# A rebuilt opening, row norms and gate tiles over both halves in a hybrid S5, convolution and ConvFFN trunk

## The chip, the cores and the metric

The kernel runs on 1 core of one Trainium2 chip. The metric is the time of one execution on the device in microseconds (us); of several runs the median is given. The core has five engines that each take their own instructions strictly in order: TensorE (PE, the matrix engine), VectorE (DVE), ScalarE (ACT), GpSimd (POOL) and SyncE (SP, which here issues DMA transfers). Engines wait for each other with semaphores. PE writes its results into PSUM, which here is cut into eight banks of 128 x 512 numbers.

## The reference, cut to what matters

The model has two layers and runs on a prompt of 1040 tokens (16 of them fixed "meta" tokens) and 8 samples of 4 tokens. Each layer has a mixer and a ConvFFN with a causal depthwise convolution of width 3. The change lies in the mixer of the first layer:

```python
xn = rms_norm(x, p['norm_mix'][l])
z = xn @ p['w_in_even'][i]                      # 1024 -> 2048
u_a, x_b, g_b, g_c = jnp.split(z, [512, 1024, 1536], axis=-1)
y_a, nh_re, nh_im = s5_scan(u_a, ...)           # complex diagonal state space, 32 groups x 64 states
y_a = jax.nn.gelu(y_a)
y_a = y_a * jax.nn.sigmoid(y_a @ w_glu + b_glu)
conv, nbuf = causal_dwconv(g_c * x_b, sbuf, p['w_sconv'][i])   # width 3
y_b = g_b * conv
out = jnp.concatenate([y_a, y_b], axis=-1) @ p['w_out_even'][i]
```

The second layer's mixer is a Conformer convolution module of width 31 with two 1024-wide products and a layer norm. Both ConvFFNs have an inner width of 2816. All is float32.

## The kernel before, in words

**Tokens.** The 1072 tokens are laid along the free dimension, features on the 128 partitions. They are cut into two halves of 512 and 560. Half 0 fills one PSUM bank; half 1 is done as two blocks of 280 in two banks.

**Products.** A float32 product is made from three faster ones. A weight tile (128 x 1024, 512 KB) is loaded by SP into `raw`, copied by ACT into its high part `wh`, and DVE or POOL subtracts to get the low part `wl` (`weight`, lines 105 to 116; a counter hands out the subtractions). The activations are split alike into `xnh` and `xnl`, with the norm's gain as a scale (`split`, lines 136 to 145). `dense` (line 118) then runs over the eight tiles of 128 input features and, for each, issues xh.wh, xl.wh and xh.wl: 24 matmuls of 512 columns for half 0, 48 of 280 columns for half 1 (line 126). The row norm is not applied before a product but when its result is read out of PSUM (`evac`, which multiplies by `rstd`).

**The opening.** `prepare` (line 275) splits each x tile, squares it on ACT, and adds the squares up on DVE (half 0) or POOL (half 1). `inv_std` then multiplies the sum by ones on PE (`nrm`, line 196), computes the inverse root on DVE, puts it on a diagonal `dg`, and PE spreads it over the partitions (`bcs`, line 213). Four tiles of `z` hold u_a; `u_tile` (line 368) makes them in the order `ORDER_U`, each tile and half on its own, and writes them to DRAM (`du`), from where they come back group by group.

**S5.** For each u tile q, `s5_const` (line 302) makes constants on DVE: `vb` with `xv` (transposed by PE, `tr`, to `ws`), the rotation table `et` with `xe`, and `oc` with `x1`, from which PE makes `kt`, which goes as `kp` to DRAM (`dk`) and comes back as Toeplitz tiles `tm`. `s5_main` (line 390) has PE make `s` from `u` and `ws`, DVE rotate it, scan it and rotate it back (`hp`, `xr`, `ss`), and PE make `y` from `tm` and `u` and from `oc` and `hp`.

**Gates.** `z_tiles` (line 500) makes one of four tiles of x_b, g_c and g_b. `z_gate` makes x_b and g_c, their product `tp` and the convolution `c`; `z_out` makes g_b, multiplies and writes the result to DRAM (`db`). Tiles 0 and 1 are done over both halves at once. Tiles 2 and 3 are done for half 0 and then again for half 1, with the weights loaded twice. `load_yb` reads all four tiles back and splits them for the output product.

**What sets the order.** The code is written in one sequence. A planner in the framework plays it through with its own costs and sets each engine's order ahead: among what is ready, what stands earlier in the code goes first. A tile can only be written when a buffer of its pool is free. The pools here are "x" (16 buffers), "xh" (32), "t" (15) and "v" (8), all of 128 x 584 numbers, and the PSUM banks: five for "mm", two for "aux", one for "cv". In the order on the chip, each engine is held to that sequence even where another instruction could go.

Of the kernel before, what the change touches and what calls it, by code (L numbers as in the profile page):

```python
# [64 lines left out]
def build(nc, tc, ctx, a):  # L65
# [52 lines left out]
    def dense(pairs, hf, blk=None):  # L118
# [3 lines left out]
        for k, (wh, wl, x) in enumerate(pairs):  # L122
            for i in range(3):
                xx = x[hf][1 if i == 1 else 0]
                for b, (t0, n_) in enumerate(blk):
                    PE.matmul(banks[b][:, :n_], wl if i == 2 else wh, xx[:, t0:t0 + n_],  # L126
                              start=(k == 0 and i == 0), stop=(k == n - 1 and i == 2))
        return banks
# [111 lines left out]
    xs = [[None, None] for _ in range(KT)]  # L240
    xraw = [[None, None] for _ in range(KT)]
    for hf in BOTH:
        for k in range(KT):
            x = xraw[k][hf] = slot("x", "x", hf)
            SY.dma_start(x, a["x"][:, k, T0[hf]:T0[hf] + TN[hf]])
            if hf == 0 and k == 5:
                wu.append(weight("w_in", 1, V))
            if hf == 1 and k == 2:
                wu.append(weight("w_in", 2, PL))
        if hf == 0:  # L250
            SY.dma_start(lpk, a["lpk"])
    bcb, bcc = slot("t", "bcb", [P, 2, GP, SI]), slot("t", "bcc", [P, 2, GP, SI])
    SY.dma_start(bcb, a["bc"][:, 0:2])
# [831 lines left out]
```

## Time and profile before

The median of three runs is 2256.58 us (2256.56 to 2257.72). The profiled execution took 2255.68 us; its span in the trace is 2253.9, at a mean granted PE clock of 0.994.

| engine | busy us | share of the span |
|---|---|---|
| PE, matmuls | 2216.1 | 98% |
| PE, weight loads (beside the matmuls) | 2007.0 | 89% |
| DVE | 1585.3 | 70% |
| ACT | 761.9 | 34% |
| POOL | 853.5 | 38% |

DMA moved 218.15 MB. `w_in` was loaded in 22 pieces of 512 KB, `du` written in 8 transfers, `u` read back in 32.

How to read what follows: a row with a start time lists one instruction, or some alike (x4), with the start and the duration in us from the start of the span; "[4.97 <-PE mm L126]" says that the engine had been idle for 4.97 us and was released by that line. A group row gives the count, the busy time, the mean duration in ns of one, and idle time ahead. Matmuls overlap, so that the distance from one start to the next is shorter than a duration. A matmul on plain float32 operands (`s`, `y`, `tr`, `kt`, `bcs`) stands in the code once and in the trace twice, except for the transposes. A window row gives busy times in one stretch of the span.

### The profile page before, as it was taken

What the parts mean: (1) busy time and instruction counts of PE and PEld (TensorE: products, weight loads), DVE (VectorE), ACT (ScalarE), POOL (GpSimd) and SP (SyncE); (2) the same over time, 40 slices, a digit from 0 to 9 for tenths busy, and PEclk for the clock granted to TensorE, in tenths of its full rate; (3) what the DMA queues carried; (4) which work ended last, traced back from release to release, by engine and by line L of the source; (5) the groups of instructions that cost most, each with busy time, mean ns of one, the idle gap of its engine ahead of it and who ended that gap; (6) DMA issues with size and microseconds to landing.
All of it is one profiled execution on the core that took longest, in us unless ns stands there. A gap on an engine that the chain in (4) does not pass through costs nothing.

```text
span 2253.9 us, 34441 instructions
## 1 busy us (share of the span) xinstructions
PE 2216.1 (98%) x13754; PEld 2007.0 (89%) x13754; DVE 1585.3 (70%) x2600; ACT 761.9 (34%) x1043; POOL 853.5 (38%) x705
## 2 busy tenths in 40 slices
PE   7999999999999999999999999999999999999997
PEld 6888888888888889999999998878888999999997
DVE  8979866544554678888886789899987455444455
ACT  5123354322332423222234423333335332322232
POOL 3212114322333434433344426455453543433342
PEclk8999999999999999999999999999999999999998
DMA  5234541333333332222223353332333323222231
GB/s 169 94 96 134 194 132 51 90 94 96 96 95 97 91 96 86 85 85 85 85 76 93 97 103 100 94 94 86 102 94 92 91 95 108 85 85 85 85 93 65
DMA packets 98400, 218.15 MB, mean 97 GB/s; under 512 B 28480, under 2 KB 44224, under 8 KB 98240
## 3 DMA queue, kind: packets, MB, share of 16 engines
q1 hardware_dynamic: 98240, 215.95, 32.5%
q8 instruction: 108, 1.77, 0.3%
q14 instruction: 52, 0.43, 0.1%
HBM read 202.49 MB, written 13.43 MB: 96 GB/s over the span
## 4 chain that ended last, share of the span: by engine, by line
PE 87%; DVE 8%; ACT 1%; DMA 1%; issue 1%; SPq 1%; DVEq 0%; ACTq 0%
PE mm L126 85%; DVE c L459 1%; DVE xr L98 1%; DVE cva L858 1%; DVE cvb L858 1%; PE bcs L213 1%; DVE xnl L144 1%; SPq L695 1%; DVE xr L970 1%; DVE sg L98 0%; DMA raw<-w_in 0%; ACT wh L110 0%; DVE wl L98 0%; PE nrm L196 0%; PE s L403 0%
## 5 line engine op out<-in xcount | busy, mean ns | idle before, releaser
L126 PE MATMUL mm<-xnh,wh 128*128 128x280 f32 (+1 forms) x2880 | 791.8, 327 | 8.6 <-ACT xnh L143 6.8
L126 PE MATMUL mm<-xnl,wh 128*128 128x280 f32 (+1 forms) x2880 | 794.6, 327 | 3.0 <-DVE xnl L144 3.0
L126 PE MATMUL mm<-xnh,wl 128*128 128x280 f32 (+1 forms) x2880 | 792.4, 327 | 0.0
L98 POOL TENSOR_TENSOR wl<-raw,wh 128x1024 fp32r<-128x1024 f32 x203 | 498.5, 2456 | 697.7 <-ACT wh L110 676.3
L110 ACT ACTIVATE wh<-raw 128x1024 fp32r<-128x1024 f32 x348 | 368.5, 1059 | 822.8 <-PE mm L126 727.6
L126 PEld LDWEIGHTS mm<-xnh,wh 128*128 128x128 f32 x2880 | 489.5, 189 | 51.5 <-ACT xnh L143 6.8
L126 PEld LDWEIGHTS mm<-xnl,wh 128*128 128x128 f32 x2880 | 488.7, 188 | 48.6 <-DVE xnl L144 4.9
L126 PEld LDWEIGHTS mm<-xnh,wl 128*128 128x128 f32 x2880 | 489.2, 189 | 42.5 <-issue 0.8
L126 PE MATMUL mm<-hh,wh 128*128 128x280 f32 (+1 forms) x1056 | 298.1, 326 | 3.0 <-DVE xr L98 3.0
L126 PE MATMUL mm<-hl,wh 128*128 128x280 f32 (+1 forms) x1056 | 299.2, 326 | 0.0
L126 PE MATMUL mm<-hh,wl 128*128 128x280 f32 (+1 forms) x1056 | 297.6, 326 | 0.0
L98 DVE TENSOR_TENSOR xr<-mm,xr 128x280 f32<-128x280 f32 (+1 forms) x336 | 166.9, 523 | 168.2 <-PE mm L126 167.9
L98 POOL TENSOR_TENSOR s<-s,g 128x512 f32<-128x512 f32 (+1 forms) x88 | 122.2, 1389 | 291.1 <-DVE g L98 201.5
L98 DVE TENSOR_TENSOR wl<-raw,wh 128x1024 fp32r<-128x1024 f32 x145 | 184.4, 1272 | 27.2 <-ACT wh L110 23.5
L126 PEld LDWEIGHTS mm<-hh,wh 128*128 128x128 f32 x1056 | 182.3, 188 | 19.8 <-DVE xr L98 4.3
L126 PEld LDWEIGHTS mm<-hl,wh 128*128 128x128 f32 x1056 | 182.3, 188 | 15.7 <-DVE hl L98 0.4
L126 PEld LDWEIGHTS mm<-hh,wl 128*128 128x128 f32 x1056 | 181.8, 188 | 15.3
L459 DVE SCALAR_TENSOR_TENSOR c<-ap,fw,c 128x576 f32<-128x576 f32 (+1 forms) x176 | 174.1, 989 | 30.3 <-ACT c L457 27.4
L98 DVE TENSOR_TENSOR hl<-s,hh 128x512 fp32r<-128x512 f32 (+1 forms) x88 | 129.6, 1472 | 86.3 <-ACT hh L140 86.1
L858 DVE SCALAR_TENSOR_TENSOR cva<-vp,w_dw,cva 128x512 f32<-128x512 f32 x240 | 179.0, 746 | 0.1
L858 DVE SCALAR_TENSOR_TENSOR cvb<-vp,w_dw,cvb 128x512 f32<-128x512 f32 x240 | 179.0, 746 | 0.0
L98 DVE TENSOR_TENSOR ap<-mm,rstd 128x32 f32<-128x32 f32 (+2 forms) x176 | 68.5, 430 | 119.1 <-PE mm L126 102.1
(206 smaller groups left out, 2002.6 us busy)
## 6 DMA issues: line engine op xcount, KB each, us to landing
raw<-w_up SPq DMA_DIRECT2D x176, 512.0 KB
raw<-w_down SPq DMA_DIRECT2D x88, 512.0 KB
raw<-w_pw SPq DMA_DIRECT2D x48, 512.0 KB
raw<-w_in SPq DMA_DIRECT2D x22, 512.0 KB
raw<-w_out SPq DMA_DIRECT2D x12, 512.0 KB
du<-up SPq DMA_DIRECT2D x8, 292.0 KB
u<-du SPq DMA_DIRECT2D x32, 73.0 KB
x<-x SPq DMA_DIRECT2D x8, 280.0 KB
```

The costliest lines, as they stand in the source:

```text
L98: return e.tensor_tensor(o, x, y, op=op)
L110: A.activation(h, raw, AF.Copy)
L126: PE.matmul(banks[b][:, :n_], wl if i == 2 else wh, xx[:, t0:t0 + n_], start=(k == 0 and i == 0), stop=(k == n - 1 and i == 2))
L144: V.scalar_tensor_tensor(l, src, scale, h.bitcast(F32), op0=MUL, op1=SUB)
L213: PE.matmul(b[:, c * w:(c + 1) * w], one1[:w], dg[:, c0 + c], start=True, stop=True)
L459: mk = V.scalar_tensor_tensor(dst[:, :n], src[:, k:k + n], w[:, k:k + 1], dst[:, :n], op0=MUL, op1=ADD)
L695: SY.dma_start(ya[:, j], dy[q][jj * SI:(jj + 1) * SI].rearrange("o g c -> g o c"))
L858: V.scalar_tensor_tensor(b, v, w, b, op0=MUL, op1=ADD)
L970: V.scalar_tensor_tensor(x, x, gam[:, 4, m:m + 1], b, op0=MUL, op1=MUL)
```

## The change

1. **Opening.** The order on ACT, DVE, SP and PE is written by hand from the start to behind the third read-out of half 1 (`manual_schedule`). Nine matmuls on a tile of ones come first on PE. The weights of the first three u tiles are loaded in halves, the first halves from ACT's queue. For half 0 the three u tiles are made together, step by step over the eight input tiles (`u_step`), in three banks. The rest follow as u0 of half 1, u1 of half 1, u3 of half 0, u2 and u3 of half 1.
2. **Norm.** x is read a second time in a row layout (`xrow`, tokens on the partitions). ACT squares each row and accumulates the sum; the squares of the column layout, the additions on DVE and POOL and the `nrm` matmuls are gone. The second norm's spread stands in the middle of u3's half 0, by a new hook in `dense`.
3. **Gate tiles.** All four are done over both halves, so that `w_in` is loaded 16 times. Tile 3's result is split at once; only tiles 0 to 2 go through DRAM. The first half of y_b is loaded behind tile 3's first half.
4. **Pools.** Pool "v" has nine buffers. The Toeplitz tiles `tm` move from "v" to "t", y_b's tiles to "t", and `kp` has a buffer of its own. The zeros `zz` and the order of some constants come later.

```diff
-NXT, NXH, NTT, NVT = 16, 32, 15, 8
+NXT, NXH, NTT, NVT = 16, 32, 15, 9
...
-    def dense(pairs, hf, blk=None):
+    def dense(pairs, hf, blk=None, hook=None):
...
+            if hook:
+                hook(k)
...
+    early = bank("warm")
+    for _ in range(9):
+        PE.matmul(early[:, :P], one1, one1, start=True, stop=True)
...
+    for q in range(3):
+        load_w(A, q, 0)
...
+    def load_rows(hf, cs):
+        w = ROWS[hf][0]
+        for c in cs:
+            for i in range(2):
+                r = xrow[hf, c, i] = slot("v", "xrow", [w, 512])
+                t0 = T0[hf] + c * w
+                SY.dma_start(r, a["xrow"][t0:t0 + w, i * 512:(i + 1) * 512])
+
+    def square_rows(hf, cs):
+        w = ROWS[hf][0]
+        for c in cs:
+            for i in range(2):
+                r = xrow.pop((hf, c, i))
+                A.activation(r, r, AF.Square, scale=1.0 / math.sqrt(D), accum_out=msq[:w, hf, c, i:i + 1])
...
+    def u_step(k):
+        for i in range(3):
+            for q in range(3):
+                w = wu[q][1 if i == 2 else 0][:, k * P:(k + 1) * P]
+                PE.matmul(ub[q], w, xs[k][0][1 if i == 1 else 0], start=(k == 0 and i == 0),
+                          stop=(k == KT - 1 and i == 2))
...
-    def prepare(hf):
-        for k in range(KT):
-            x = xraw[k][hf]
-            xs[k][hf] = split(x, "xn", hf, gam[:, 0, k:k + 1])
-            sq = slot("t", "sq", hf) if hf == 0 else x
-            A.activation(sq, x, AF.Square)
-            if k:
-                tt(acc, acc, sq, ADD, (V, PL)[hf])
-            else:
-                acc = sq
-        rstd.append(inv_std(acc))
...
-        kp = slot("v", "kp", [P, P])
+        kp = sm.tile([P, P], F32, tag="kp", name="kp", bufs=1)
...
-        tm = [slot("v", "tm", [P, 4, P]) for _ in range(2)]
+        tm = [slot("t", "tm", [P, 4, P]) for _ in range(2)]
...
+        if i == 3:
+            ybs[i][hf] = split(g, "ybs", hf)
+        else:
+            SY.dma_start(db[i][:, T0[hf]:T0[hf] + TN[hf]], g)
...
+    u01 = full_k(wu[0], xs, 1)
+    u11 = full_k(wu[1], xs, 1)
...
+    u30 = dense([wslice(w3, k) + (xs[k],) for k in range(KT)], 0, hook=lambda k: k == 3 and rstd.append(inv_spread(dg)))
+    u_out(0, 1, u01)
+    u_out(3, 0, u30)
+    u_out(1, 1, u11)
+    order.__exit__(None, None, None)
+    u_out(2, 1, full_k(wu[2], xs, 1))
+    u_out(3, 1, full_k(wu[3], xs, 1))
...
-    for i in (2, 3):
-        z_tiles(i, (0,))
-    load_yb(0, "xh")
-    for i in (2, 3):
-        z_tiles(i, (1,))
+    z_tiles(2)
+    z_tiles(3)
```

In the rows of the orders below a number behind a name tells one tile from another, and the engines that a row waits for stand behind it (DMAHW is a DMA transfer).

The first place is the start of PE's order. Before:

```order
L126 MATMUL mm_356<-xnh_170,wh_76 128x512 [waits Activation_49]
L126 MATMUL mm_356<-xnl_171,wh_76 128x512 [waits DVE_49]
L126 MATMUL mm_356<-xnh_170,wl_77 128x512
L126 MATMUL mm_356<-xnh_176,wh_76 128x512 [waits Activation_49]
L126 MATMUL mm_356<-xnl_177,wh_76 128x512 [waits DVE_49]
```

And now:

```order
L253 MATMUL warm_102<-one1_74 128x128 [waits Pool_49]
L253 MATMUL warm_102<-one1_74 128x128 x8
L316 MATMUL mm_126<-xnh_181,wh_113 128x512 [waits Activation_49]
L316 MATMUL mm_127<-xnh_181,wh_116 128x512 [waits Activation_49]
L316 MATMUL mm_128<-xnh_181,wh_120 128x512 [waits Activation_49]
L316 MATMUL mm_126<-xnl_182,wh_113 128x512 [waits DVE_49]
L316 MATMUL mm_127<-xnl_182,wh_116 128x512
L316 MATMUL mm_128<-xnl_182,wh_120 128x512
L316 MATMUL mm_126<-xnh_181,wl_114 128x512 [waits DVE_49]
L316 MATMUL mm_127<-xnh_181,wl_117 128x512 [waits DVE_49]
L316 MATMUL mm_128<-xnh_181,wl_121 128x512 [waits DVE_49]
L316 MATMUL mm_126<-xnh_200,wh_113 128x512 [waits Activation_49]
```

An input tile is used for nine matmuls in three banks instead of three in one.

The second place is PE at the S5 products of q2 (`s_1929` before, `s_1961` now). Before, gate matmuls stand between them and the y products:

```order
L403 MATMUL s_1929<-u_1900,ws_1530 64x138 [waits Activation_49]
L403 MATMUL s_1929<-u_1900,ws_1530 64x138 x3
L126 MATMUL mm_2480<-xnl_258,wh_2467 128x280
L126 MATMUL mm_2479<-xnh_257,wl_2468 128x280
...
L126 MATMUL mm_2601<-xnl_276,wh_2595 128x280
L450 MATMUL y_1977<-hp_1935,oc_1597 128x138 [waits DVE_49,Activation_49]
L450 MATMUL y_1978<-hp_1935,oc_1597 128x138
L126 MATMUL mm_2600<-xnh_275,wl_2596 128x280
```

And now (`y_2009` is of q2; `tr_2055`, `kt_2130`, `s_2154` and `y_2220` are of q3; `mm_2384` is the second half of the gate g_c of z tile 2, half 1):

```order
L485 MATMUL s_1961<-u_1932,ws_1562 64x138 [waits Activation_49]
L485 MATMUL s_1961<-u_1932,ws_1562 64x138 x3
L526 MATMUL y_2009<-u_1931,tm_1998 128x138 [waits DMAHW4_49,Activation_49]
...
L532 MATMUL y_2009<-hp_1967,oc_1629 128x138 [waits DVE_49,Activation_49,Pool_49]
...
L404 MATMUL tr_2055<-ident_77,vb_2045 128x128 [waits DVE_49,Activation_49]
...
L434 MATMUL kt_2130<-oc_2121,bd_832 32x128 [waits DVE_49,Activation_49]
...
L485 MATMUL s_2154<-u_2142,ws_2053 64x138 [waits DMAHW7_49,Activation_49]
...
L526 MATMUL y_2220<-u_2142,tm_2209 128x138 [waits DMAHW0_49,Activation_49]
...
L127 MATMUL mm_2384<-xnh_305,wh_2263 128x280 [waits DVE_49]
```

Where "..." stands there are only further rows of the same S5 work. 115 gate and output matmuls stood between `s` and the first `y` on `hp`; now none does before `mm_2384`.

The third place is DVE from the last gate result of z tile 1 on. Before, the first evacuations of z tile 2 (`xb_2235`, `gc_2236`) stand right behind it:

```order
L98 TENSOR_TENSOR gb_1843<-gb_1843,c_1804 128x32
L98 TENSOR_TENSOR xb_2235<-mm_2237,rstd_245 128x512 [waits PE_49]
L98 TENSOR_TENSOR wl_2335<-raw_2332,wh_2334 128x1024 [waits DMAHW0_49,Activation_49]
L98 TENSOR_TENSOR vb_1521<-pk2_768,bb_792 128x512 [waits DMAHW6_49]
L98 TENSOR_TENSOR xv_1520<-pk2_768,bb_792 128x512 [waits DMAHW3_49,DMAHW5_49,DMAHW2_49,DMAHW1_49]
L98 TENSOR_TENSOR vb_1522<-pk2_768,bb_792 128x512
L98 TENSOR_TENSOR gc_2236<-mm_2263,rstd_245 128x512 [waits PE_49]
```

And now:

```order
L99 TENSOR_TENSOR gb_1875<-gb_1875,c_1836 128x32
L99 TENSOR_TENSOR wl_2448<-raw_2445,wh_2447 128x1024 [waits DMAHW4_49,Activation_49]
L99 TENSOR_TENSOR vb_1553<-pk2_800,bb_824 128x512 [waits DMAHW2_49]
...
L99 TENSOR_TENSOR hp_1967<-et_1575,ss_1941 128x4x130 [waits DMAHW7_49,DVE_49]
...
L99 TENSOR_TENSOR vb_2045<-pk2_800,bb_824 128x512 [waits PE_49]
...
L99 TENSOR_TENSOR xe_2069<-et_2068,trig_795 128x4x2 [waits DVE_49]
L99 TENSOR_TENSOR xb_2267<-mm_2269,rstd_333 128x512
L99 TENSOR_TENSOR gc_2268<-mm_2295,rstd_333 128x512 [waits DMAHW5_49,DMAHW6_49,DMAHW0_49,PE_49]
```

Between the two ends stand the constants of q2, its rotations and scans, and the constants of q3; `xb_2267` reads z tile 2's first bank behind all of them.

More of the change, by code (lines that the diff above doesn't have):

```diff
@@ L223, in inv_std @@
         return r
+    order = tc.manual_schedule(engines={ET.Activation, ET.DVE, ET.SP, ET.PE})
+    order.__enter__()
+    gam = load("gam", [P, 5, KT])
     warm = small("warm", [P, 1])
+    one1 = small("one1", [P, P])
+    PL.memset(one1, 1.0)
     PL.memset(warm, 0.0)
-    A.activation(warm, warm, AF.Copy)
-    gam = load("gam", [P, 5, KT])
-    wu = [weight("w_in", 0, V)]
-    pk = slot("t", "pk", [P, 36, GP])
-    npk = [0]
-    def carve(n):
-        npk[0] += n
-        return pk[:, npk[0] - n:npk[0]]
-    lpk = carve(3)
-    lre, lim, ldt = [lpk[:, i] for i in range(3)]
-    xs = [[None, None] for _ in range(KT)]
-    xraw = [[None, None] for _ in range(KT)]
-    for hf in BOTH:
-        for k in range(KT):
[L244 to L253, printed above, removed]
-    SY.dma_start(bcc, a["bc"][:, 2:4])
-    h0 = load("h0", [P, 2, GP, NS])
-    dmat = load("dmat", [P, 4])
-    dmask = load("dmask", [P, SI])
     ident = small("ident", [P, P])
@@ L265, in build @@
         PL.memset(mult[:, 8 + n:9 + n], float(8 << n))
-    one1 = small("one1", [P, P])
-    PL.memset(one1, 1.0)
+    msq = small("msq", [P, 2, 5, 2])
+    early = bank("warm")
+    for _ in range(9):
+        PE.matmul(early[:, :P], one1, one1, start=True, stop=True)
+    xs = [[None, None] for _ in range(KT)]
+    xraw = [[None, None] for _ in range(KT)]
+    xrow, wraw, wu = {}, {}, []
+    for q in range(3):
+        if q < 2:
+            r = wp.tile([P, 1024], F32, tag="raw", name="raw", bufs=2)
+            wraw[q] = [r[:, :512], r[:, 512:]]
+        else:
+            wraw[q] = [slot("t", "raw", [P, 512]) for _ in range(2)]
+        wu.append([wp.tile([P, 1024], F32R, tag=t, name=t, bufs=WB) for t in ("wh", "wl")])
@@ new lines, in load_w, with w_split, load_x @@
+    def load_w(e, q, i):
+        e.dma_start(wraw[q][i], a["w_in"][q][:, i * 512:(i + 1) * 512])
+    for q in range(3):
+        load_w(A, q, 0)
+    A.activation(warm, warm, AF.Copy)
+    def w_split(q, i, lo, hi, low=True):
+        r = wraw[q][i][:, lo:hi]
+        h, l = [w[:, i * 512 + lo:i * 512 + hi] for w in wu[q]]
+        A.activation(h, r, AF.Copy)
+        if low:
+            tt(l, r, h.bitcast(F32), SUB)
+    def load_x(hf, ks):
+        for k in ks:
+            x = xraw[k][hf] = slot("x", "x", hf)
+            SY.dma_start(x, a["x"][:, k, T0[hf]:T0[hf] + TN[hf]])
@@ new lines, in build @@
+    load_x(0, (0, 1))
+    for q in range(3):
+        load_w(SY, q, 1)
+        load_x(0, (2 + q,))
+    load_rows(0, (0, 1))
+    load_x(0, (5,))
+    load_rows(0, (2, 3))
+    load_x(0, (6, 7))
+    load_x(1, range(KT))
+    w_split(0, 0, 0, P, False)
+    split_x(0, (0,))
+    w_split(0, 0, P, 512, False)
+    tt(wu[0][1][:, :512], wraw[0][0], wu[0][0][:, :512].bitcast(F32), SUB)
+    w_split(1, 0, 0, 512)
+    w_split(2, 0, 0, 512)
+    u_step(0)
+    split_x(0, (1, 2))
+    u_step(1)
+    w_split(0, 1, 0, 512)
@@ new lines, in build, with carve @@
+    split_x(0, (3,))
+    u_step(2)
+    w_split(1, 1, 0, 512)
+    split_x(0, (4,))
+    u_step(3)
+    w_split(2, 1, 0, 512)
+    square_rows(0, (0, 1))
+    u_step(4)
+    split_x(0, (5,))
+    u_step(5)
+    square_rows(0, (2, 3))
+    split_x(0, (6, 7))
+    u_step(6)
+    u_step(7)
+    split_x(1, (0,))
+    dg = rows_inv(0)
+    split_x(1, (1, 2))
+    rstd = [inv_spread(dg)]
+    pk = slot("t", "pk", [P, 36, GP])
+    npk = [0]
+    def carve(n):
+        npk[0] += n
+        return pk[:, npk[0] - n:npk[0]]
@@ new lines, in build @@
+    lpk = carve(3)
+    lre, lim, ldt = [lpk[:, i] for i in range(3)]
+    SY.dma_start(lpk, a["lpk"])
+    bcb, bcc = slot("t", "bcb", [P, 2, GP, SI]), slot("t", "bcc", [P, 2, GP, SI])
+    raw3 = wp.tile([P, 1024], F32, tag="raw", name="raw", bufs=2)
+    SY.dma_start(raw3, a["w_in"][3])
+    load_rows(1, range(4))
+    SY.dma_start(bcb, a["bc"][:, 0:2])
+    SY.dma_start(bcc, a["bc"][:, 2:4])
+    h0 = load("h0", [P, 2, GP, NS])
+    dmat = load("dmat", [P, 4])
+    dmask = load("dmask", [P, SI])
@@ L541, in build @@
     V.tensor_scalar(mag, em1, 1.0, None, op0=ADD)
+    zz = slot("v", "zz", [P, 240 - P])
+    PL.memset(zz, 0.0)
+    for q in range(4):
+        SY.dma_start(dk[q][:, P:240], zz)
     nearest(kk, aim, 1.0 / (2 * PI))
```

80 lines of the change are left out of this document (49 added, 31 removed).

## The prediction

> **What bounds the kernel now.** I read the page's busy time first, then the windows of the opening, the waits of TensorE (PE), and the rows of VectorE (DVE) one by one.
>
> ```profile
> span 2253.9 us, 34441 instructions
> PE 2216.1 (98%) x13754; PEld 2007.0 (89%) x13754; DVE 1585.3 (70%) x2600; ACT 761.9 (34%) x1043; POOL 853.5 (38%) x705
> ...
> 5.00:10.00 5.00, 2.64 (x5) 1.78 (x6) 3.79 (x5) 4.80 (x7) 0.00 (x0) 1.00 1.04 396
> 15.00:20.00 5.00, 5.00 (x23) 4.05 (x22) 4.98 (x11) 4.84 (x8) 2.04 (x1) 1.00 1.06 391
> 30.00:35.00 5.00, 3.44 (x27) 3.21 (x26) 5.00 (x22) 1.94 (x3) 2.93 (x2) 1.00 0.00 0
> 35.00:40.00 5.00, 1.29 (x8) 0.83 (x7) 4.97 (x15) 1.70 (x3) 3.55 (x10) 0.83 0.00 0
> 40.00:45.00 5.00, 3.81 (x19) 3.73 (x19) 3.34 (x15) 0.60 (x1) 0.00 (x0) 0.50 0.15 21
> 45.00:50.00 5.00, 3.07 (x14) 3.10 (x15) 4.80 (x16) 1.00 (x3) 0.00 (x0) 0.50 0.21 84
> 50.00:55.00 5.00, 5.00 (x34) 5.00 (x33) 4.71 (x21) 1.71 (x3) 0.63 (x4) 0.80 0.31 121
> sum 75.00, PE 58.70 PEld 52.70 DVE 61.15 ACT 30.87 POOL 25.85; mean PE 3.91 PEld 3.51 DVE 4.08 ACT 2.06 POOL 1.72
> ...
> 75.00:100.00 25.00, 25.00 (x167) 21.94 (x165) 25.00 (x89) 4.68 (x8) 3.99 (x5) 1.00 0.29 88
> 100.00:125.00 25.00, 25.00 (x169) 20.49 (x168) 24.88 (x78) 4.56 (x8) 2.77 (x5) 1.00 0.36 101
> ```
>
> A window row gives its length, then the busy us of PE, weight loads, DVE, ScalarE (ACT) and POOL, the granted clock, the DMA share and GB/s. PE idles 37.8 us in the whole span (2253.9 - 2216.1), and 16.3 of them lie in the first 75 us (75.00 - 58.70). So the kernel is PE's work plus its holes. The opening is the largest hole; from 35 to 55 us it also runs at a clock of 0.50 to 0.83. Behind it PE is full, but from 75 to 125 us DVE is full as well (25.00 and 24.88 of 25). That second fact decides this case: PE cannot be brought forward much without running into DVE.
>
> **The opening, step by step.**
>
> ```profile
> 10.03 0.63 PE L126 MATMUL mm<-xnh,wl 128*128 128x512 f32 x1
> 10.45 0.63 PE L126 MATMUL mm<-xnh,wh 128*128 128x512 f32 x1
> 11.19 0.39 PE L126 MATMUL mm<-xnh,wl 128*128 128x512 f32 x1
> 11.42 0.40 PE L126 MATMUL mm<-xnh,wh 128*128 128x512 f32 x1
> ...
> 50.60 0.43 PE L126 MATMUL mm<-xnh,wh 128*128 128x280 f32 x1
> 50.83 0.43 PE L126 MATMUL mm<-xnl,wh 128*128 128x280 f32 x1
> 52.00 0.30 PE L126 MATMUL mm<-xnh,wh 128*128 128x280 f32 x1
> 52.26 0.29 PE L126 MATMUL mm<-xnh,wl 128*128 128x280 f32 x1
> ...
> 74.69 1.24 DVE L98 TENSOR_TENSOR up<-mm,rstd 128x140 f32<-128x140 f32 x6 [4.97 <-PE mm L126]
> ```
>
> Start to start, a 512-column matmul takes 0.42 us, then 0.23 at full clock, and a 280-column one 0.23, then 0.13 (two in 0.26). Before, the u phase ends where its last result is read, at 74.7.
>
> After the change, PE first runs nine warm-up matmuls on constants, so the clock is full when data comes. The first step needs three half weights and one x tile, 1.0 MB; at the 390 GB/s of the rows between 5 and 20 us, starting near 2 us, they land near 5, and with one split PE starts at about 5.5. Step 0 also waits for three low weight splits and ends near 8.4. Seven more steps of nine matmuls, 9 x 0.23 = 2.1 us each, end at 23.2. Each step needs 256 KB of x and at most half a weight: 2.1 us at 390 GB/s carry 0.8 MB, so the steps are PE's. Then come the norm's spread (0.7), u01 and u11 with 48 matmuls of 0.13 each (12.4, and 1.5 of waits for x's second half), u30 with 24 of 0.23 and a second spread (6.8), and u21 and u31 (12.4): 57.0. **Gain 74.7 - 57.0 = 17.7 us.**
>
> The doubled reading of x speaks against it: the second copy in rows is 4.4 MB more, and the sum of all transfers up to the last of them is about 12.2 MB, so it lands near 2 + 12.2/0.39 = 33, with issue gaps 36. It is needed for the second norm at about 40, inside u30. Its cover is 4 us; were it gone, u30's middle waits. I take 15 (first tile late and waits for the half-1 tiles) to 19.5 (no waits) as the bounds.
>
> [...]
>
> The removed x squares, DVE additions and norm matmuls count in this gain, not again. The six weight loads fewer (22 to 16) take 6 x 512 KB of DMA and 6 splits from engines that PE does not wait for here; I cost them at nothing.
>
> **The first new wait: z tile 0.** In the order after, the first evacuation xb of z0 (which frees a bank that the second 280-column group of gc needs) stands on DVE behind the constants of q0 and q1. That DVE stretch holds kp of q0, which needs the kt matmuls, and those stand on PE among and behind 64 matmuls of 280 columns. PE leaves u at 57.0. Two 512-column groups take 24 x 0.23 each, with eight transposes 12.2 us; 64 matmuls of 0.13, four transposes and the eight kt rows of the order (16 in the trace) take 9.5. So kt ends at 78.7, ACT copies it, and DVE goes on at 79.2. DVE then has 8.8 us of constants until xb: six 576-column products (4.0) and some 28 small ones (4.8).
>
> ```profile
> 79.05 0.74 DVE L98 TENSOR_TENSOR x<-pk,bcc 128x576 f32<-128x576 f32 x1
> 79.72 0.74 DVE L98 TENSOR_TENSOR oc<-pk,bcc 128x576 f32<-128x576 f32 x1
> 83.33 0.25 DVE L98 TENSOR_TENSOR xe<-et,trig 128x16 f32<-128x16 f32 x2
> 83.50 0.68 DVE L98 TENSOR_TENSOR xb<-mm,rstd 128x512 f32<-128x512 f32 x1
> ...
> 203.41 2.88 DVE L459 SCALAR_TENSOR_TENSOR c<-tp,w_sconv,c 128x512 f32<-128x512 f32 x1
> ...
> 203.30 2.44 POOL L98 TENSOR_TENSOR wl<-raw,wh 128x1024 fp32r<-128x1024 f32 x1 [1.97 <-ACT wh L110]
> ...
> L319 PE MATMUL tr<-ident,vb 128*128 128x128 f32 x32 | 4.6, 272 | 0.0
> L349 PE MATMUL kt<-oc,bd 128*32 128x128 f32 x64 | 3.4, 285 | 0.0
> ```
>
> A transpose costs 0.14 and a kt matmul 0.05 (4.6/32, 3.4/64, for four constants). A 576-column product costs 0.67 start to start; a small one is between 0.09 (two xe in 0.17) and about 0.35 (my estimate for 256 columns from the 0.2 of a 128-column one, quoted below). So xb is done at 88.7, while PE, with four transposes, eight matmuls, kt and eight s more, reaches the waiting group at about 82: **a stall of 6.8 us**. A POOL split beside a DVE instruction adds about 2 (2.88 where 512 columns take 0.7 in the rows around), so 9 is the upper bound; 1 is the lower, if DVE gets past kp without waiting.
>
> **The second new wait: z tile 2.** This is the largest term. In the order before, 115 gate and output matmuls stand on PE between the last s of q2 and the y matmuls that read its scan; the trace shows those 16 to 20 us covered:
>
> ```profile
> 203.31 0.69 PE L403 MATMUL s<-u,ws 128*64 128x138 f32 x8
> 219.91 0.51 PE L450 MATMUL y<-hp,oc 64*128 64x138 f32 x4
> 223.13 0.98 PE L450 MATMUL y<-hp,oc 64*128 64x138 f32 x12 [1.09 <-ACT hp L431]
> 226.98 1.10 PE L444 MATMUL y<-u,tm 128*128 128x138 f32 x8
> ...
> 208.62 0.69 DVE L98 TENSOR_TENSOR hp<-et,ss 128x520 f32<-128x520 f32 x1
> 209.33 0.69 DVE L98 TENSOR_TENSOR hp<-hp,xr 128x520 f32<-128x520 f32 x1
> 211.41 1.38 DVE L421 TENSOR_TENSOR_SCAN ss<-pk,hp 128x130 f32<-128x130 f32 x4
> 228.48 0.69 DVE L98 TENSOR_TENSOR vb<-pk,bb 128x512 f32<-128x512 f32 x1
> 249.25 0.49 DVE L98 TENSOR_TENSOR xe<-et,trig 128x128 f32<-128x128 f32 x2
> ```
>
> In the order after, nothing but S5 work stands there: s, y of q2, transposes, kt and s of q3, the first y of q3, and only then a gate matmul (the second half of gc in z2, half 1). All five banks of the pool "mm" wait at that point for z2's evacuations, and DVE has these behind the rotation of q2 (11 instructions of 520 columns at 0.61 and 8 scans at 0.33: 9.4 by these rows) and the whole constant of q3 (six vb/xv products of 0.60, six 576-column ones of 0.67, and the et/xe steps, 7.3 together: 14.9). In the order before, the constants' vb stood behind z2's evacuations, since a buffer of the pool "v" came free late; now the Toeplitz tiles have left that pool and it has nine buffers, and the constants come first.
>
> So from the last s of q2, DVE needs 9.4 + 14.9 = 24.3 us, then 0.7 for xb, 0.5 for ACT's copy ahead, and about 3.5 for one or two POOL splits: 29. PE has work for 9.5 of it (16 y<-u of 0.13, 32 y<-hp of 0.075, eight transposes, 16 kt, 32 s of 0.07 and 8 y<-u of q3, with each count as the trace shows it for one q): **a stall of 19.5 us**; 16 without POOL, 23 with every split in it. Nothing can go into the hole, since PE takes its instructions in order.
>
> **The clock.** The page's gap from 35 to 49 us was followed by 2.9 us at half clock (49.05 to 52.0 in the spacing above). A stall of 20 us should be followed by the same: 1.5 us lost, 0 to 2.5. [...]
>
> **What the change takes away later.** z3's gate goes to its split without DRAM, and z2 and z3 run over both halves. Before, PE's small holes from 220 to 340 us are:
>
> ```profile
> 200.00:225.00 25.00, 23.91 (x183) 22.51 (x184) 24.03 (x43) 8.24 (x16) 6.43 (x6) 1.00 0.45 136
> 275.00:300.00 25.00, 23.33 (x188) 21.99 (x187) 10.95 (x19) 7.70 (x13) 4.77 (x2) 1.00 0.77 233
> ```
>
> They are 2.8 us (1.1 and 1.7); most should go, and some of what other windows lose, -2 (0 to -3), as DVE has then finished its constants early. The loads of the first half of y_b stand behind the 22 ya transfers on SP and land just before PE wants them.
>
> **Sum.** -17.7 + 6.8 + 19.5 + 1.5 - 2 = +8.1, on the profiled execution's own 2255.68 (its span of 2253.9 and 1.8 around it), which is 0.9 below the median of 2256.58. I forecast **2264 us**. With all lower ends together it would be -19.5 + 1 + 16 + 0 - 3 = -5.5 (2250), with all upper ones -15 + 9 + 23 + 2.5 = +19.5 (2275).
>
> **Rivals.** First, *the gain stands*, the other side: DVE passes kp of q0 unhindered since ACT copies it early, z0 then costs PE 1 us, and at z2 no POOL split lies in the chain. -18.5 + 1 + 16 - 3 = -4.5, and with 3 us more of the stall covered by y work that I timed short, 2248. It decides where z0's stall is under 2 us. For it: before, POOL splits came some 13 us apart at 200. Against it: kt has a fixed place on PE, and DVE is in order. Chance 0.10. Second, *gain and stalls cancel*: z0's stall is 3, z2's 17, and the clock is not lost: -17.7 + 3 + 17 - 2 = +0.3, 2256. For it: DVE enters z2 early and only the chain behind s counts. Chance 0.25. Third, *the opening does not do what it says*: the doubled x, the row squares on ACT and the splits of the half weights starve PE, so that it gains 8 to 10 instead of 17.7, while DVE is late anyway, so z0's stall falls to 3: -9 + 3 + 19.5 + 1.5 = +15, 2271. For it: ACT was busy 4.8 of 5 us at 15 to 20 already, and it now has weight halves and row squares. Against it: the x squares left it. Chance 0.12.
>
> **How the numbers follow.** The forecast gets the rest, 0.53, with its own range of 2258 to 2270. A measurement of this kernel tells about 0.2%, 4.5 us, from no change. Slower (above 2261): 0.48 of the forecast's 0.53 and all of the third, 0.60. Faster (below 2252): 0.10. Within: 0.30. The range reaches down to the cancelling case and up to the third, 2252 to 2273.
>
> **What would show it.** In the profile after: the first reader of the last u matmul at 55 to 60, where a time over 62 means the third rival; a PE wait of 3 to 9 us near 82 to 89 at the bank of z0's gc, released by DVE xb; PE idle 16 to 23 us between 175 and 206, released by DVE's hp, vb, oc and xb and by ACT's kp and the Toeplitz loads behind it, with a granted clock below 1 just after. If PE is full from 150 to 220, the forecast is wrong, and DVE was ahead where I have it behind. If the stalls are there and the time is still below 2252, the planner's order later gives back what I put at 2 us.

## The result: slower by 1.3%

The changed kernel takes 2287.22 us (median of four runs, 2286.09 to 2287.59), the kernel before 2257.15 (2256.56 to 2259.71). The ratio is 1.0132, with a 95% interval of 1.0116 to 1.0148. The direction was forecast, the size was not: the profiled execution's span went from 2253.9 to 2285.8 us, +31.9 where the sum said +8.1, and the time lies above the range.

The page of the changed kernel, its span and each engine's busy time:

```profile
span 2285.8 us, 34436 instructions
PE 2238.8 (98%) x13754; PEld 2025.0 (89%) x13754; DVE 1621.8 (71%) x2596; ACT 761.8 (33%) x1061; POOL 807.6 (35%) x694
```

PE runs the same 13754 matmuls and is still busy 98% of the span. Its idle time rose by only 9.2 us (2285.8 - 2238.8 = 47.0, from 37.8). The other 22.7 us are busy time: the same matmuls took longer. The page's first lines cannot say why; the windows can. In the changed kernel (columns as in the prediction's windows, the granted clock being the third from the end):

```profile
75.00:100.00 25.00, 19.86 (x151) 16.95 (x150) 21.45 (x94) 4.73 (x9) 3.17 (x7) 0.83 0.21 54
100.00:125.00 25.00, 25.00 (x147) 21.89 (x147) 24.36 (x61) 4.68 (x10) 4.45 (x3) 0.96 0.39 112
175.00:200.00 25.00, 17.04 (x135) 14.02 (x134) 16.88 (x41) 4.13 (x11) 2.38 (x1) 0.81 0.15 45
200.00:225.00 25.00, 20.36 (x105) 15.42 (x106) 17.88 (x72) 5.19 (x12) 1.77 (x6) 0.57 0.24 68
```

Before, PE was full from 75 to 100 and lost 1.1 us from 200 to 225, all at a clock of 1.00. Now there are two holes, each with a clock below 1: one in z tile 0 (75 to 100) and one in z tile 2 (175 to 225). From 200 to 225 PE counts 20.36 us as busy, but for 105 records where it had 183: it works at 0.57 of its clock. The same kernel's longest waits of PE between 75 and 350 us (total, times, longest). The first and the third are of the hole at z tile 2, the second of the one at z tile 0:

```profile
PE y L532 <- ACT hp L513: 5.6, 1, 5.6
PE kt L434 <- DVE oc L99: 4.6, 1, 4.6
PE y L526 <- DMA tm<-dk: 3.6, 2, 1.9
```

Taking the start of one and the same piece of work in both traces, stage by stage, the whole difference is placed:

| stage, on PE | before | change | difference | forecast |
|---|---|---|---|---|
| start to the end of the u phase (74.7 and 65.3 us) | 74.7 | 65.3 | -9.4 | -17.7 |
| z tile 0, its hole and the half clock in and after it | | | +9.0 | +6.8 |
| z tile 2, the same | | | +27.6 | +21.0 (19.5 and 1.5 of clock) |
| the rest up to the first product that reads yah (a remainder) | | | -1.0 | -2 |
| from there to the first product that reads hh | 130.8 | 130.0 | -0.8 | 0 |
| from there to the last one that reads hh or hl | 1800.0 | 1806.8 | +6.8 | 0 |
| tail | | | -0.3 | 0 |
| sum | | | +31.9 | +8.1 |

`yah` is the high part of the gated S5 result, `hh` and `hl` are the two parts of a ConvFFN's inner activations. A hole's entry is the time in which PE did not run its work at full clock: at z2, 35.2 us from the end of q2's last `s` products (they start at 188.07 and take 0.6) to the gate product `mm_2384` (223.89), with 9.5 of S5 work at full clock taken off, and 1.9 of half clock behind it. Of the 35.2 us PE was idle for only 12.3; the other 22.9 went on work that takes 9.5 at full clock.

### The profile page after: what moved, and what is told of

Read it like the earlier page. It is cut to its first block, busy times and chain, and to the rows that moved or that the text cites. A ratio compares the mean times of both kernels' runs of the same rounds, so it can differ in the third digit from the quotient of the medians.

```text
span 2285.8 us, 34436 instructions
## 1 busy us (share of the span) xinstructions
PE 2238.8 (98%) x13754; PEld 2025.0 (89%) x13754; DVE 1621.8 (71%) x2596; ACT 761.8 (33%) x1061; POOL 807.6 (35%) x694
## 4 chain that ended last, share of the span: by engine, by line
PE 84%; DVE 11%; DMA 2%; issue 1%; ACT 1%; SPq 0%; POOL 0%; ACTq 0%; DVEq 0%
PE mm L127 82%; DVE c L541 1%; DVE xnl L147 1%; DVE xr L99 1%; DVE cva L965 1%; DVE cvb L965 1%; DVE wl L99 1%; PE bcs L220 1%; PE y L532 1%; DVE hl L99 1%; DVE cv L99 1%; DVE sq L99 1%; DMA x<-x 0%; DVE xr L1077 0%; DVE yal L99 0%
## 5 line engine op out<-in xcount | busy, mean ns | idle before, releaser
L127 PE MATMUL mm<-xnh,wl 128*128 128x280 f32 (+1 forms) x2856 | 782.8, 326 | 0.0
L99 POOL TENSOR_TENSOR wl<-raw,wh 128x1024 fp32r<-128x1024 f32 x199 | 489.8, 2462 | 681.7 <-ACT wh L111 680.9
L111 ACT ACTIVATE wh<-raw 128x1024 fp32r<-128x1024 f32 x338 | 358.3, 1060 | 784.5 <-PE mm L127 695.7
L541 DVE SCALAR_TENSOR_TENSOR c<-ap,fw,c 128x576 f32<-128x576 f32 (+1 forms) x176 | 240.5, 1366 | 59.0 <-ACT c L539 56.1
L99 DVE TENSOR_TENSOR wl<-raw,wh 128x1024 fp32r<-128x1024 f32 (+1 forms) x146 | 220.1, 1508 | 32.2 <-ACT wh L111 30.0
L99 POOL TENSOR_TENSOR s<-s,g 128x512 f32<-128x512 f32 (+1 forms) x88 | 127.3, 1446 | 228.6 <-DVE g L99 137.4
L99 DVE TENSOR_TENSOR ap<-mm,rstd 128x32 f32<-128x32 f32 (+2 forms) x176 | 68.6, 431 | 121.1 <-PE mm L127 120.0
L875 ACT ACTIVATE s<-c 128x512 f32<-128x512 f32 (+1 forms) x88 | 56.3, 640 | 237.9 <-DVE c L541 236.2
```

The lines of the kernel that those rows point to most:

```text
L99: return e.tensor_tensor(o, x, y, op=op)
L111: A.activation(h, raw, AF.Copy)
L541: mk = V.scalar_tensor_tensor(dst[:, :n], src[:, k:k + n], w[:, k:k + 1], dst[:, :n], op0=MUL, op1=ADD)
L875: A.activation(s[:, :n], c[:, :n], AF.Silu)
```

## The experiments

The main question was what makes the two holes. The **pool theory**: the Toeplitz tiles `tm` left the pool "v", so the constants of the later S5 parts no longer wait for a buffer of it, and DVE makes them ahead of the z tiles' evacuations. The **gate theory**, its rival: running z2 and z3 over both halves, with the fourth gate split in place, moves the gate products away. A third: the shorter opening itself brings PE to DVE's constants too early. The second question was where 8.3 us of the opening's gain went; the third, what the +6.8 from hh on are.

**The change with `tm` back in "v".**

```diff
-        tm = [slot("t", "tm", [P, 4, P]) for _ in range(2)]
+        tm = [slot("v", "tm", [P, 4, P]) for _ in range(2)]
```

> The changed kernel with one edit undone: the Toeplitz tiles tm come from pool v again (still nine buffers). Theory P (the pool of tm lets the constants of q2 and q3 ahead of z tile 2's evacuations on DVE): the stretch of 35 us between the last s of q2 and the next gate matmul, of which 9.5 is S5 work, goes, and the half clock behind it: 2287 - 28 = 2259, or 2250 if the wait at z tile 0 goes as well. Theory G (the gate tiles over both halves are the cause): the stall stays, 2280 or more. Theory O (the opening is the cause, its late norm): 2280 or more as well, with the stall moved.

Measured: 2252.57 us beside 2256.53 before, ratio 0.9981 [0.9972, 0.9991], 34.6 us below the change. Its windows:

```profile
75.00:100.00 25.00, 25.00 (x172) 22.45 (x171) 23.01 (x74) 5.31 (x9) 3.77 (x7) 1.00 0.21 61
175.00:200.00 25.00, 25.00 (x188) 22.02 (x187) 22.29 (x74) 6.75 (x11) 5.82 (x7) 1.00 0.26 81
200.00:225.00 25.00, 25.00 (x176) 22.55 (x175) 20.55 (x36) 4.05 (x10) 1.69 (x5) 1.00 0.34 107
```

Both holes are gone, z tile 0's too, and the clock stays at 1.00. The gates still run over both halves here and the opening is the new one, so neither can make the holes without the move. DVE's rows show the order behind it: here the first `vb` of q3 starts at 219.4 us, behind z tile 2's first evacuation `xb` (204.5); in the changed kernel it is the other way round (199.3 and 221.0).

**The kernel before, with `tm` alone moved to "t"** (the edit above, reversed, on the kernel before).

> The kernel before with one edit: tm in pool t, v still with eight buffers. Theory P: PE stands without gate matmuls between s and y of q2 here too, a hole of 16 to 26 us and a half clock of some 2 us behind it: 2257 + 20 to 28 = 2277 to 2285. Theories G and O: no change, 2257.

Measured: 2286.99 us, 1.0133 [1.0118, 1.0148]: the change's time, from one word, and just above the expected 2277 to 2285. Its windows, and PE's rows in the hole:

```profile
175.00:200.00 25.00, 22.27 (x133) 16.91 (x131) 17.93 (x65) 7.51 (x13) 4.91 (x4) 1.00 0.37 109
200.00:225.00 25.00, 17.15 (x82) 12.24 (x82) 18.16 (x58) 4.24 (x12) 0.27 (x3) 0.52 0.27 81
225.00:250.00 25.00, 22.80 (x137) 20.13 (x135) 23.61 (x58) 6.45 (x10) 5.56 (x6) 0.79 0.59 189
```

```profile
199.45 0.47 PE L444 MATMUL y<-u,tm 128*128 128x138 f32 x2 [2.49 <-DMA tm<-dk]
```

The hole of z2 is there from 197 on, again with half the clock, though the old opening and the old order of the z tiles stand; q3's first `vb` (208.0) is ahead of z2's `xb` (229.4) here too. That this kernel's pool "v" keeps its eight buffers also settles a detail: not the ninth buffer but the absence of `tm` from the pool makes the new order. From 75 to 100 us PE is full here (25.00 of 25, clock 1.00), so the hole there needs the new opening as well as the move.

**The new opening alone** (the gate tiles, the pools of `tm` and `kp` and the order of the z tiles as before).

The part of the edit that sets the order of the z tiles:

```diff
-    z_tiles(2)
-    z_tiles(3)
...
+    for i in (2, 3):
+        z_tiles(i, (0,))
+    load_yb(0, "xh")
+    for i in (2, 3):
+        z_tiles(i, (1,))
```

> The changed kernel's opening (with nine buffers in v for its row tiles) on the gate tiles, pools of tm and kp, and order of the kernel before. If the opening keeps what it wins by the end of the u phase (9.4 us: 74.7 to 65.3), 2257 - 9 = 2248; if DVE, full from 75 to 125 us before, takes it back at z tile 0, 2252 to 2257; theory O: 2260 or more.

Measured: 2263.50 us, 1.0029 [1.0020, 1.0039]; a clear miss. Neither hole is there (PE is busy 25.00 of 25 us from 75 to 100, from 175 to 200 and from 200 to 225), so the third theory, that the shorter opening makes them, falls. PE reaches the first product that reads the gates' halves `ybsh` at 235.6 us, 14.8 ahead of the kernel before, but by the first product on hh it is 1.8 behind (438.0 for 436.2). Another 5.6 us are lost in the long stretch from there on (1805.6 for 1800.0), which is taken up below. PE's waits from 225 to 340 us in it, and one row:

```profile
PE mm L127 <- DVE xr L99: 5.1, 2, 3.7
PE mm L127 <- ACT yah L808: 2.2, 2, 1.6
```

```profile
259.24 0.80 PE L127 MATMUL mm<-ybsh,wh 128*128 128x512 f32 x1 [3.73 <-DVE xr L99]
```

DVE still makes q3's constants there (`et`, `xe` up to 261 us in its rows), and the evacuation `xr` waits among them; a window from 250 to 275 us has PE at 20.20 of 25 and a clock of 0.86. PE had run ahead of the S5 work and waited for it later. So in this kernel the earlier PE won nothing while DVE's constants were still in the way, and this run also shows that the opening's gain is no fixed sum that can be added to others.

**The gates alone** (the kernel before with z2 and z3 over both halves and tile 3 split in place; a part of the edit).

```diff
+        if i == 3:
+            ybs[i][hf] = split(g, "ybs", hf)
+        else:
+            SY.dma_start(db[i][:, T0[hf]:T0[hf] + TN[hf]], g)
...
```

> The kernel before with the gate tiles of the change alone: all four over both halves, six weight loads fewer, tile 3 split without DRAM; pools and opening as before. Theory P: PE does not wait for what is saved, 2254 to 2258, the small holes of 3 us between 220 and 340 us may go. Theory G: a hole at z tile 2 and 2270 or more.

Measured: 2259.19 us, 1.0010 [1.0000, 1.0019]. The gate theory falls: this part costs at most 4 us by itself.

**The deal of the weight splits.** A counter `state["n"]` deals the low halves of the weights to DVE and POOL; the new opening takes some splits out of the count, so that from there on every split may go to the other engine. With `tm` in "v", the counter was set back to 0.5, where it stood in the kernel before, when the order of the opening ends:

```diff
     order.__exit__(None, None, None)
+    state["n"] = 0.5
```

> e1 (the change with tm back in v) with one number more: the counter that deals the low weight splits out between DVE and POOL starts the gate tiles at 0.5 instead of 0, as it stood in the kernel before, where u3's weights had advanced it. In the change and in e1 the stretch behind the first ConvFFN's start is 6.7 us longer than before (1806.5 for 1799.8). Theory F (the phase of that counter, which swaps DVE and POOL for every later weight): the stretch falls back to 1800 to 1802, and the time to 2246 to 2249. Rival (the new opening shifts something else, or the plan scatters by chance): it stays at 1805 to 1807, 2251 to 2254.

Measured: 2254.38 us, 0.9990 [0.9982, 0.9999], not better than the 2252.57 without it. The stretch from hh to the last product on hh or hl took 1804.4 us (1806.8 without the edit), where the theory had expected 1800 to 1802. But one place answers. It lies between two spreads of row norms, late in the kernel. The kernel before, the change and this one:

```profile
1708.43 1.26 PE L213 MATMUL bcs<-dg,one 112*128 112x112 f32 x10
...
1837.11 1.27 PE L213 MATMUL bcs<-dg,one 112*128 112x112 f32 x10
```

```profile
1735.46 1.37 PE L220 MATMUL bcs<-dg,one 112*128 112x112 f32 x10 [0.85 <-DVE dg L99]
...
1868.08 1.26 PE L220 MATMUL bcs<-dg,one 112*128 112x112 f32 x10
```

```profile
1705.99 1.37 PE L220 MATMUL bcs<-dg,one 112*128 112x112 f32 x10 [0.77 <-DVE dg L99]
...
1834.70 1.26 PE L220 MATMUL bcs<-dg,one 112*128 112x112 f32 x10
```

128.7 us, 132.6 and 128.7: at this place the swapped deal costs some 4 us. Over the whole stretch only 2.4 of them are left, so other places take a part back. Shifted only ahead of the first ConvFFN (the line `state["n"] = (state["n"] + 0.5) % 1` in front of it):

> e1 with the counter of the weight splits moved on by half a step only behind the output product, ahead of the first ConvFFN; all up to there is e1's order. Theory F (the phase of the counter makes the stretch behind 5 to 7 us longer, as e5 has half shown): the stretch between the second norm of the first ConvFFN (at 392.2 us in e1) and the last norm (2237.1) falls from 1844.9 to 1835 to 1839, and the time from 2252.6 to 2243 to 2247. Rival (e5's stretch was shorter by other orders ahead of it): 1843 to 1846, 2251 to 2254.

Measured: 2250.19 us, 0.9967 [0.9955, 0.9978], 2.4 below the run with `tm` in "v" alone, though the two intervals overlap, and above the 2243 to 2247 that were expected. The place takes 128.8, yet the whole stretch still takes 1806.0: what is won at this place is lost at others. So the deal sets what this place costs, and it is not shown that it makes the +6.8.

**Warm-up matmuls: 16, and none** (both on the run with the counter set back; the second leaves out the nine warm-ups, which compute nothing that is used).

```diff
-    for _ in range(9):
+    for _ in range(16):
```

> e5 with 16 warm-up matmuls instead of 9, so that PE runs without a gap until the first data. In the change the clock was still half from 6.1 to 13.0 us behind the nine. If the gap of 0.9 us and the wait of 1.6 behind step 0 are what keeps the clock low: full from about 8.6, the u phase ends 2 us earlier, 2 us off e5's time. If the warm-ups do not count for the clock at all: half clock to 12 or 13 as before, no change or up to 1 us later by the longer row of warm-ups.

> e5 without warm-up matmuls. If the nine are worth nothing: the clock turns full at 11 to 13 us and the time stays within 1 us of e5. If they shorten the half clock: up to 2 us slower.

Measured: 2255.27 us, 0.9995 [0.9986, 1.0003], and 2255.15, 0.9996 [0.9987, 1.0006]. The time says nothing; the traces do. The opening of the changed kernel on PE:

```profile
0.99 4.21 PE L253 MATMUL warm<-one 128*128 128x128 f32 x18 [0.99 <-POOL warm L241]
...
8.60 0.79 PE L316 MATMUL mm<-xnh,wh 128*128 128x512 f32 x1 [0.77 <-ACT wh L276]
...
11.75 1.48 PE L316 MATMUL mm<-xnh,wh 128*128 128x512 f32 x3
```

And with 16:

```profile
0.99 5.20 PE L253 MATMUL warm<-one 128*128 128x128 f32 x32 [0.99 <-POOL warm L241]
...
9.04 0.86 PE L316 MATMUL mm<-xnl,wh 128*128 128x512 f32 x3
```

Three 512-column matmuls take 1.48 us after nine warm-ups and 0.86 after sixteen. (The granted clock of the windows reads 1.00 from 9 to 13 us in the changed kernel and does not show this half clock; the spacing does.) Still, nine were not always worth nothing. In four of the eight traces with nine, the first product came at full clock, and the clock fell again; in the other four it was half from the start. The run with `tm` in "v" is one of the first four (a single 512-column matmul lasts 0.50 us at full clock and 0.79 at half):

```profile
6.80 0.50 PE L316 MATMUL mm<-xnh,wh 128*128 128x512 f32 x1 [0.48 <-ACT wh L276]
8.35 0.50 PE L316 MATMUL mm<-xnh,wh 128*128 128x512 f32 x1 [1.04 <-ACT wh L276]
...
9.70 1.48 PE L316 MATMUL mm<-xnh,wl 128*128 128x512 f32 x3
```

Either way, full clock came to stay only between 10.4 and 13.8 us with nine, and at 14.3 with none; with sixteen it was there from the first product on in all three traces. What makes the difference between the four traces and the other four is not shown. That 16 bring no time has its reason in the next run.

**The last row tile early.** The second norm's last tile of 112 rows is loaded with the other four, out of the pool "t", on the run with the counter set back.

```diff
-                r = xrow[hf, c, i] = slot("v", "xrow", [w, 512])
+                r = xrow[hf, c, i] = slot("t" if c == 4 else "v", "xrow", [w, 512])
...
-    load_rows(1, range(4))
+    load_rows(1, range(5))
...
-    load_rows(1, range(4, 5))
```

> e5 with the last row tile of x's second half loaded right behind the four others, ahead of the S5 constants' inputs (its two buffers come from pool t). In the change it is issued at 37.5 and 38.7 us, lands at 41 and 43, and the second norm's spread waits 3.0 us (4.6 in e1) with a half clock behind it. Theory N (the late last row tile holds the norm): the wait falls below 1 us and the u phase ends 4 to 6 us earlier; time 4 to 6 below e5. Rival (the queue of transfers or ACT's squares are the limit): the wait stays over 2.5 us, within 2 us of e5.

Measured: 2245.73 us, 0.9958 [0.9945, 0.9970], 8.65 below the same kernel without the edit, more than the 4 to 6 that were expected. The waits of PE at the second spread, in the changed kernel, with 16 warm-ups, and here:

```profile
PE bcs L220 <- DVE dg L99: 3.0, 1, 3.0
```

```profile
PE bcs L220 <- DVE dg L99: 5.8, 2, 5.4
```

```profile
PE bcs L220 <- DVE dg L99: 0.8, 1, 0.8
```

The spread had waited for the last row tile. In the runs with no, nine and sixteen warm-ups (all with the counter set back) it starts at 50.1, 50.4 and 50.2 us, whatever the clock was before: that is why full clock from the first product on won nothing. The cause, in SP's and ACT's rows of the changed kernel:

```profile
37.48 0.33 SPq L295 DMA_DIRECT2D xrow<-xrow  x1
37.93 0.35 SPq L108 DMA_DIRECT2D raw<-w_in  x1
38.65 0.33 SPq L295 DMA_DIRECT2D xrow<-xrow  x1
```

```profile
43.16 0.63 ACT L302 ACTIVATE xrow<-xrow 112x512 f32<-112x512 f32 x1 [1.53 <-DMA xrow<-xrow]
```

The last halves are issued at 37.5 and 38.7, with 512 KB of weights between. They stand on SP behind the inputs of the S5 constants and need a "v" buffer that ACT's squares free; the edit changed both, and which of the two held them is not separated.

**Both, and with the late shift.** The early row tile with 16 warm-ups; then `tm` in "v", the early row tile, 16 warm-ups and the shift ahead of the first ConvFFN only:

> e8 with 16 warm-ups. In e6 the 16 brought the full clock from the first step on (matmuls of 0.23 us from 8.7 on, instead of half clock to 12 or 13), but the second norm's wait took it back. If that was the only reason, the 2.0 to 2.3 us now show: the u phase ends 2 us before e8's, 2243 to 2244. If the last row tile is again what is waited for, even now, under 1 us.

> All together: tm in v, the last row tile early, 16 warm-ups, the counter moved on ahead of the first ConvFFN. If the gains add: e10's time less 4 to 6 for the norm and 2 for the clock, 2237 to 2242. If DVE, 100% busy behind the opening, takes the earlier start back: 2243 to 2248.

Measured: 2248.14 us, 0.9961 [0.9948, 0.9973], and 2247.47, 0.9959 [0.9945, 0.9972]. With 2245.73 above, these three are one result: some 0.4% faster than the kernel before, 1.7 to 1.8% faster than the change. The expected further gain of the warm-ups did not come; in the first of the two the u phase ends only 0.3 us sooner than without them (61.5 for 61.7), and PE waits 2.5 us for DVE's split `xnl` in the first 350 us where it had waited 0.5.

**The change itself with the early row tile** (`tm` stays in "t").

> The changed kernel itself (tm in t) with the last row tile early and nothing else. The u phase ends 4 to 6 us earlier. If PE's stalls at z tiles 0 and 2 are set by chains that start with PE's own work (kt, the last s of q2), the gain stays: 2287 - 5 = 2282. If DVE's load ahead of them sets them, they grow by what the opening wins: 2285 to 2288.

Measured: 2282.17 us, 1.0113 [1.0100, 1.0127], 5 below the change, though the two intervals overlap. Of its waits:

```profile
PE y L531 <- ACT hp L512: 5.5, 1, 5.5
PE kt L433 <- DVE oc L99: 4.6, 1, 4.6
```

Both holes are as large as in the change, though PE starts its first transposes 3.4 us sooner (68.6 for 72.0): coming earlier or later by so much does not move them.

**Both kernels once more, unedited.**

> The kernel before, unedited, for another profile. If the stretch belongs to the kernel: 1799 to 1801 us from the first to the last matmul on hh or hl. If it scatters by execution: anything up to 1806.

> The changed kernel, unedited, for another profile. If the stretch belongs to the kernel: 1806 to 1808. If it scatters: 1800 to 1807. The hole at z tile 2 (188 to 224 us) should stand within 2 us of the first profile in either case, as both ends hang on orders that are fixed.

Measured: 2257.43 and 2285.99 us. From hh to the last product on hh or hl the kernel before took 1802.9 us where it had 1800.0, the change 1806.7 where it had 1806.8. So 2.9 of the +6.8 are inside the scatter of the kernel before. The other runs lie between 1802.0 and 1806.8. The hole at z tile 2 stood within 1.2 us of where it had stood (from the last `s` of q2 at 186.9 to the gate product at 223.2).

## Why the prediction was right and wrong

**Bound, place and sign: right.** "PE cannot be brought forward much without running into DVE" holds, and both holes stand where they were named. At z2 the releasers are among those that were named: hp, kp and the Toeplitz loads. At z0 DVE's stretch is the one that was named, late behind kp of q0, but PE's wait stands one step ahead: at kt of q1 behind DVE's oc (4.61 us), and not at the bank of gc behind xb. The cause given for z2, `tm` out of the pool "v", is shown by taking it away and by doing it alone. The rival in which the gain stands fails: DVE waits for kp of q0 until 87.35. So does the cancelling one, whose stalls of 3 and 17 us became 9.0 and 27.6.

**The opening, -17.7, failed: -9.4**, the first half of the third rival. Two steps broke. "PE first runs nine warm-up matmuls on constants, so the clock is full when data comes": it was half until about 13 us, and the third half weight came at 8.60, so the eight steps end at 27.0 and not 23.2 (3.8 us). "Its cover is 4 us; were it gone, u30's middle waits": it was gone. The tile is not late because 12.2 MB take that long: the rows above show it issued late. u30 with its spread took 11.6 us for 6.8 (4.8). The rows also moved more slowly than the 390 GB/s of the sum. In the changed kernel, while x tiles were loaded and while the rows of x's second half were, both at a full DMA share:

```profile
22.00:24.00 2.00, 2.00 (x11) 1.59 (x10) 1.70 (x12) 0.56 (x1) 0.00 (x0) 1.00 1.05 408
30.00:32.00 2.00, 1.98 (x15) 1.76 (x15) 2.00 (x4) 2.00 (x4) 0.00 (x0) 1.00 1.01 295
```

The third rival's second half, a smaller z0 hole, did not come: it needs DVE to be late while PE is not, and both came later together.

**z tile 0: +6.8 for the hole right, partly by luck; the clock left out.** The rows of the changed kernel, PE and then DVE:

```profile
88.30 0.29 PE L127 MATMUL mm<-xnh,wl 128*128 128x280 f32 x1
93.20 0.66 PE L434 MATMUL kt<-oc,bd 128*32 128x128 f32 x8 [4.61 <-DVE oc L99]
...
97.20 0.60 PE L127 MATMUL mm<-xnh,wh 128*128 128x280 f32 x1
```

```profile
87.35 0.83 DVE L99 TENSOR_TENSOR kp<-kp,dm 128x16 f32<-128x16 f32 x1 [3.55 <-ACT kp L436]
...
96.24 0.69 DVE L99 TENSOR_TENSOR xb<-mm,rstd 128x512 f32<-128x512 f32 x1
```

From kp to xb DVE took 8.9 us where the prediction had 8.8. PE's pause is 8.8 us, less 1.8 of S5 work: 7.0. That it meets the 6.8 is in part luck: PE left the u phase 8.3 us later than forecast, and DVE came past kp 8.2 us later (87.35 for 79.2), so that the error of the opening fell out. The clock then stayed at half until 101.9; the 18 gate matmuls from 97.20 on came 0.233 us apart where the same ones take 0.128, 2.0 us more in all. The prediction's sum has no term for that: its 1.5 us of half clock stand behind z2's hole alone.

**z tile 2: +21.0, measured 27.6; the step that failed is "PE has work for 9.5 of it", at full clock and beside a DVE that never stops.** The prediction let DVE run 24.3 us without a stop. DVE in the changed kernel:

```profile
209.30 0.29 DVE L99 TENSOR_TENSOR et<-et,xe 128x32 f32<-128x32 f32 x2
216.64 0.18 DVE L99 TENSOR_TENSOR kp<-kp,dm 128x16 f32<-128x16 f32 x1 [7.05 <-ACT kp L436]
...
221.04 0.69 DVE L99 TENSOR_TENSOR xb<-mm,rstd 128x512 f32<-128x512 f32 x1
```

It stood 7.05 us for kp of q3. kp needs PE's kt, and that stands on PE behind all of q2's y, the transposes and `s` of q3. PE was late with these: it had waited 5.62 us for hp, and from 190.6 to 218.0 us it had half the clock, so that eight `y<-u` took 2.53 us, and 2.74 at the end of the hole, where the row of the kernel before has 1.10. A smaller part are loads of `u` that SP issued behind others:

```profile
202.48 7.29 SPq L536 DMA_DIRECT2D dy<-y  x2
209.87 5.02 SPq L477 DMA_DIRECT2D u<-du  x8
```

The two dy writes wait on SP for the result of y of q2 and hold these loads back; PE's own waits for them are 1.55 us (1.11 and 0.44). The chain goes PE, ACT, DVE, PE, ACT, DVE, DMA, PE, in series where the prediction had PE's 9.5 us beside DVE's.

```profile
190.40 2.53 PE L526 MATMUL y<-u,tm 128*128 128x138 f32 x8 [1.64 <-DMA tm<-dk]
198.54 0.83 PE L532 MATMUL y<-hp,oc 64*128 64x138 f32 x4 [5.62 <-ACT hp L513]
...
221.51 2.74 PE L526 MATMUL y<-u,tm 128*128 128x138 f32 x8 [1.94 <-DMA tm<-dk]
```

The wait that ended last is not the one for xb either, which was done at 221.7: the Toeplitz loads of q3, which follow kp, held PE's `y` until 221.51, and the gate product came behind it. So from the last `s` to the end of xb it took 33.0 us where the prediction had 29 (DVE's own work 25.2 for 24.3, the 7.05 on top, and none of the 3.5 put in for POOL splits, so that one error hid half of the other), and 2.2 more to the gate product. That is 6.2 us; with 0.4 more of half clock behind the hole the term was too small by 6.6. The place and the cause were right. The sign "PE idle 16 to 23 us" was not met: PE was idle for 12.3 us, and the half clock, which the prediction put only behind the hole, made the rest.

**Later: -2 right (-1.0, within its 0 to -3), the remainder wrongly 0.** From hh on the change lost 6.8 us. The swapped deal of the splits costs some 4 at one place, but the run that shifts it back there keeps the long stretch (1806.0); 2.9 is no more than the scatter between two executions of the kernel before. What the rest of the 6.8 is made of stays open.

## What to carry to other kernels

A full pool is also a brake on the order: a tile that leaves it can let work that nobody waits for yet pass in front of the evacuations that free PSUM banks, so after each edit to a pool one reads what then stands ahead of the first evacuation. Price a hole as one chain in series over all engines and queues, with PE's share of it at half clock, as it was here (a granted clock of 0.50 from 191 to 217 us in the changed kernel). And a gain in an opening is only what the next wait leaves of it: the early row tile paid because it moved that wait, the warm-ups alone did not.
